# Rotation tables of a recurrence: built in one array from powers 1 to 64, the negative half copied backwards

## The chip, the cores and the metric

The kernel runs on one core of a Trainium2 chip. The metric is the device time in microseconds of one execution of the whole program; lower is better.

## The reference, cut to what matters

One layer of an encoder with 1024 prompt and 256 sample tokens, all in float32: a feed-forward half step, a mixing sublayer of two head groups, a second feed-forward half step. One head group is a diagonal complex recurrence (S5), forward and backward in time:

```python
ar = mag * jnp.cos(lam_im * step)
ai = mag * jnp.sin(lam_im * step)
...
_, _, hr, hi = lax.associative_scan(_complex_linear_combine, (a_r, a_i, bur, bui), reverse=reverse, axis=0)
return jnp.einsum('lgp,ghp->lgh', hr, c_re) - jnp.einsum('lgp,ghp->lgh', hi, c_im)
```

The kernel cuts the tokens into chunks of 8: 128 chunks for the prompt and 32 for the sample. It takes the rotation out of the state from chunk to chunk, so that what is scanned has a real decay. For that it needs a table of cosine and sine of (chunk number x angle) for each of the 32 groups and 2 directions.

## The kernel before, in words

The program is one stream of work whose stages overlap. The first feed-forward half is done in two parts: four token tiles first (function `ffn`), then the six remaining prompt tiles (`ffn1_halves`, which calls `gated` and `Down.run`). `gated` goes over 22 slices of the hidden width. For each it makes seven block products (`p1` to `p7`) of twelve TensorE matmuls of 384 columns each (line 1435), into two sets of three PSUM banks in turn. Around the matmuls VectorE adds results out of PSUM (line 1456), ScalarE copies and applies the activation (1468, 1474, 1504), VectorE multiplies (1497, 1505). The weights of the next slices are split into a high and a low part by ScalarE (line 200) and VectorE (line 201), and GpSimd forms sums of weight blocks ahead of that (line 1403).

The preparation of the recurrence, `s5_mats`, is a generator that is run in turns with that part: `weave((fb, 33), (s5_mats(...), 102))` advances whichever of the two has the smaller share of its units behind it (33 and 102 units). Its first part makes the tables, in four passes of eight group pairs. A pass doubles the table seven times: `cmul` (lines 453 to 458, six VectorE operations) turns entries 0 to n-1 into entries n to 2n-1, for n = 1, 2, ..., 64, with cosine in one array and sine in another. Then ScalarE copies the first 32 entries behind the 128 (line 595), VectorE clears eight entries (596), ScalarE makes the negated sine (598), and ScalarE's queue issues eight stores of the finished arrays to DRAM (601). There is one buffer each for cosine, sine and negated sine, so the next pass writes them when the stores have landed. After each doubling and each pass stands a `yield 2`, so the tables take 64 of the 102 units. The second part makes the matrices of the recurrence (lines 605 to 676; VectorE operations on line 577, TensorE on 627, 649, 661 and 666). It first takes buffers that the tables have given back.

The order within each engine's queue is fixed when the program is built: each queue runs its instructions in that order, and an instruction that waits holds those behind it. Instructions of the tables may be placed ahead of their turn where their inputs are ready, and in the trace they are. `s5_prep`, which runs during the first part of the feed-forward half, makes the powers of two of the rotation by which the doublings multiply (lines 547 to 567).

Of the kernel before, what the change touches and what calls it, by code (L numbers as in the profile page):

```python
# [12 lines left out]
AF = mybir.ActivationFunctionType  # L13
ALU = mybir.AluOpType

D = 1024
DFF = 2816
NFT = DFF // 128
# [29 lines left out]
def bc(ap, axis, n):  # L48

    v = ap.unsqueeze(axis)  # L50
    shape = list(v.shape)
    shape[axis] = n
    return v.to_broadcast(shape)
# [396 lines left out]
def cmul(K, outr, outi, ar, ai, br, bi, t):  # L450

    V = K.nc.vector
    V.tensor_tensor(out=outr, in0=ar, in1=br, op=ALU.mult)
    V.tensor_tensor(out=t, in0=ai, in1=bi, op=ALU.mult)
    V.tensor_tensor(out=outr, in0=outr, in1=t, op=ALU.subtract)
    V.tensor_tensor(out=outi, in0=ar, in1=bi, op=ALU.mult)
    V.tensor_tensor(out=t, in0=ai, in1=br, op=ALU.mult)
    V.tensor_tensor(out=outi, in0=outi, in1=t, op=ALU.add)


def s5_prep(K, A, keep, banks):

    nc = K.nc
    V = nc.vector
    TT = lambda o, a, b, op: V.tensor_tensor(out=o, in0=a, in1=b, op=op)
# [67 lines left out]
    b01, b23, t = K.new(2, 64, 16), K.new(2, 64, 16), K.new(64, 16)  # L533
# [13 lines left out]

    yield 4

    tn = K.new(7, 2, 32)  # L550
    er, ei = tn.v[:, :, 0], tn.v[:, :, 1]
    for src, dst in ((e8r, er[:, 0]), (e8i, ei[:, 0])):
        ps = banks.get(32)
# [2 lines left out]
        nc.scalar.copy(out=dst, in_=ps)  # L556
    V.tensor_scalar(out=ei[:, 0, 16:32], in0=ei[:, 0, 16:32], scalar1=-1.0, scalar2=None, op0=ALU.mult)
    u = tq.v[:, 0, 0:32]
    for j in range(6):
        TT(er[:, j + 1], er[:, j], er[:, j], ALU.mult)  # L560
        TT(u, ei[:, j], ei[:, j], ALU.mult)
        TT(er[:, j + 1], er[:, j + 1], u, ALU.subtract)
        V.scalar_tensor_tensor(out=ei[:, j + 1], in0=er[:, j], scalar=2.0, in1=ei[:, j], op0=ALU.mult, op1=ALU.mult)
# [8 lines left out]
def s5_mats(K, A, keep, scr, cfg):  # L572


    nc = K.nc
    V = nc.vector
    TT = lambda o, a, b, op: V.tensor_tensor(out=o, in0=a, in1=b, op=op)
    g = lambda k: A[k][0]
    turn = K.new(7, 2, 32)
    nc.sync.dma_start(out=turn.v, in_=keep["turn"])  # L580
    er, ei = turn.v[:, :, 0], turn.v[:, :, 1]
    c_, s_, n_, tm = (K.ring(1, 8, n) for n in (160, 160, 160, 64))
    for j in range(0, 32, 8):
        d, q = divmod(j, 16)
        c, s, t = c_.get(), s_.get(), tm.get()
        V.memset(c[:, :, 0:1], 1.0)
        V.memset(s[:, :, 0:1], 0.0)
        for lev in range(7):
            n = 1 << lev
            cmul(K, c[:, :, n:2 * n], s[:, :, n:2 * n], c[:, :, 0:n], s[:, :, 0:n],  # L590
                 bc(er[:, lev, j:j + 8], 2, n), bc(ei[:, lev, j:j + 8], 2, n), t[:, :, 0:n])
            yield 2

        for v in (c, s):
            nc.scalar.copy(out=v[:, :, 128:160], in_=v[:, :, 0:32])
            V.memset(v[:, :, 127 + d:128 + d], 0.0)
        n = n_.get()
        nc.scalar.activation(out=n, in_=s, func=AF.Copy, scale=-1.0)
        for half, v, src in ((0, 0, c), (1, 0, c), (0, 1, n), (1, 1, s)):
            for gg in range(2):  # L600
                nc.scalar.dma_start(out=scr["tab"][half * 64:half * 64 + 64, q:q + 8, v, gg, d], in_=src[gg * 64:gg * 64 + 64])
        yield 2
    for r in (c_, s_, n_, tm, turn):
        r.free()

    banks, bank1 = Banks(K, cfg["prep"][:-1]), Banks(K, cfg["prep"][-1:])
    bs = K.new(2, 64, 16)
# [6 lines left out]
    for b in range(4):  # L614
        gv = gw.get()
        for d in (1, 0):
# [14 lines left out]
            for q in range(0, 8, 4):  # L631
                dg, gg = d * 32 + b * 8 + q, b * 8 + q

                def powers(lo, hi, rev):
                    r, i = (p[:, lo:hi, dg:dg + 4] for p in (pwr, pwi))
                    if rev:
                        r, i = r[:, ::-1], i[:, ::-1]
                    return tuple(bc(v.rearrange("p k g -> p g k"), 3, 16) for v in (r, i))

                iv, tv = inj.get(), tmp.get()[:, :, 0:8]  # L640
                r, i = powers(0, 8, d == 0)
# [12 lines left out]
                r, i = powers(0, 9, d == 1)  # L654
# [19 lines left out]
        for s in range(8):  # L674
            nc.sync.dma_start(out=scr["mat"][s * 16:s * 16 + 16, b * 8:b * 8 + 8, 4].rearrange("h g x -> g h x"),
                              in_=gv[:, 7 - s:15 - s].rearrange("p t h -> p (t h)"))
# [950 lines left out]
def weave(*gens):  # L1627

    live = [[0.0, n, g] for g, n in gens]
    while live:  # L1630
        w = min(live, key=lambda w: w[0] / w[1])
        try:
            w[0] += next(w[2]) or 1
        except StopIteration:
            live.remove(w)
# [7 lines left out]
def emit(ctx, tc, nc, A, dbg=None):  # L1643
    K = Ctx(ctx, tc, nc)
    V = nc.vector
    g = lambda k: A[k][0]
    dp = ctx.enter_context(tc.tile_pool(name="dr", bufs=1, space=bass.MemoryType.DRAM))
    shapes = {"mat": (128, 32, 5, 128), "tab": (128, 16, 2, 2, 2, 160), "u": (512, 8, 160), "g": (512, 8, 160),
              "rate": (2048,), "b": (128, 2, 64, 16), "turn": (128, 7, 2, 32), "h": (NFT, 128, 1024), "h1": (NFT, 128, 768), "x2": (128, 8, D)}
    for nm in NAMES:  # L1650
        L, NT, R = PARTS[nm]
        shapes.update({"spec_" + nm: (2, 2, L // R // 128, 128, 2, R, 256), "x1_" + nm: (128, NT, D), 
# [1 line left out]
    scr = {k: dp.tile(list(s), F32, name="scr_" + k) for k, s in shapes.items()}  # L1654
# [46 lines left out]
    def filter_spectra(ids):  # L1701

        FC = filt_consts(K, A)
        yield from filters(K, A, "sample", FC, scr, ids, {})
        yield from s5_prep(K, A, scr, Banks(K, ids[-2:]))
        yield from filters(K, A, "prompt", FC, scr, ids, {})

    out, x1T = {}, {}
# [16 lines left out]
    def ffn1_halves(N, first, tail, turn):  # L1725

        tb, src = Banks(K, (4, 5, 6, 7)), tokens(A["x_prompt"][0], "prompt")
        X = Blocks(K, N // 2, False)
        X.make(X.NAMES[0:2])
        xs = [K.new(2, D) for _ in range(N // 2)]  # L1730
        for j, x in enumerate(xs):
            for i in range(2):
                nc.sync.dma_start(out=x.v[:, i], in_=src[:, first + 2 * j + i])
            X.even(x.v, j, tb)
        G = GateUp(K, g("ffn1_w_gate"), g("ffn1_w_up"), True)
        G.load()
        yield 0.01
        G.early(0)
        G.parts(0)
        X.make(X.NAMES[2:])  # L1740

        def begin():
            G.sums(0, 0)
            G.sums(0, 1)
            G.load()
            G.load()
            for j, x in enumerate(xs):
                X.odd(x.v, j, tb)
                x.free()
            G.early(1)  # L1750

        dn = Down(K, g("ffn1_w_down"), scr["h1"], N)
        xr = []

        def spare(n):

            X.free(GateUp.OPS[n][1])
            if n in (1, 2):
                dn.load()
            elif n == 6:  # L1760
                xr.append(Parts(K, N, D))
                for s in range(N):
                    nc.sync.dma_start(out=xr[0].at(s), in_=src[:, first + s])

        yield from gated(K, X, G, scr["h1"], ((0, 1, 2), (3, 4, 5)), begin, spare, True)

        def done(s):
            nc.sync.dma_start(out=scr["x1_prompt"][:, first + s], in_=xr[0].at(s))
            turn(xr[0], s)

        yield from dn.run(xr[0], g("ln1_g"), g("ln1_b"), range(6), done, tail=tail)
        xr[0].free()

    fb = ffn1_halves(6, 2, to_mix, turn1)
# [7 lines left out]
    nc.sync.dma_start(out=gains[:, 0:4], in_=g("ssm_norm_g").rearrange("(k p) -> p k", p=128))  # L1782
    nc.sync.dma_start(out=gains[:, 4:8], in_=g("hy_norm_g").rearrange("(k p) -> p k", p=128))
    weave((fa, 33), (filter_spectra((4, 5, 6, 7)), 183))
    weave((fb, 33), (s5_mats(K, A, scr, scr, dict(prep=(6, 7))), 102))


    xs = load_x([(scr["x1_sample"], s) for s in range(2)])
# [8 lines left out]
    x2, x2T, yT = {}, {}, {nm: [] for nm in NAMES}  # L1797
# [231 lines left out]
```

## Time and profile before

| | us |
|---|---|
| median of 3 runs (lowest, highest) | 2573.36 (2571.69, 2576.63) |
| the profiled execution's own time | 2577.11 |
| its span, first to last instruction | 2575.3 |

The profile is of one execution. TensorE is PE (weight loads are PEld), VectorE is DVE, ScalarE is ACT, GpSimd is POOL. Starts are microseconds from the span's start. A line number is that of the kernel; a helper's line stands for all who call it. "idle before" is time in which the engine had nothing running just before the instruction, and what ended it stands behind it. PEclk is the clock that was granted to TensorE, as a share of the full 2.4 GHz.

### The profile page before, as it was taken

The page shows a single profiled execution, that of the slowest core. Times are in us where ns is not written, and L with a number is a line of the kernel's source. Part 1 is how long each engine was busy: PE and PEld are TensorE (multiplying, and loading weights), DVE is VectorE, ACT ScalarE, POOL GpSimd, SP SyncE. Part 2 cuts the span into 40 slices and gives each one's busy share as a digit, 9 for nine tenths or more (in the row PEclk, how much of TensorE's full clock was granted, in tenths as well). Part 3 has the DMA queues.
Part 4 walks back from the last instruction along what each step waited for, and adds up shares of the span by engine and source line. Part 5 has one row for each costly group of instructions (what it writes and reads, how often), then busy time and mean ns, then how long its engine had stood idle before and what let it go on. Part 6 is the DMA issues. An engine that isn't in the chain of part 4 may idle for free.

```text
span 2575.3 us, 32433 instructions
## 1 busy us (share of the span) xinstructions
PE 2485.9 (97%) x12605; PEld 2119.3 (82%) x12605; DVE 1897.0 (74%) x2873; ACT 867.3 (34%) x1291; POOL 221.4 (9%) x158
## 2 busy tenths in 40 slices
PE   8999999889999999999999999999989999999998
PEld 6777777779999988788888878899768888888887
DVE  6887777689886697657896788788986566556437
ACT  5434443323333332123444313333332222223200
POOL 0000000244343100000000000000230000000001
PEclk9999999999999999999999999999999999999999
DMA  7333232444563464445556654565433223244301
GB/s 206 114 117 94 94 93 84 155 118 131 152 168 97 166 208 144 147 135 156 172 173 189 223 196 140 168 189 160 140 112 95 77 78 95 74 149 186 130 35 66
DMA packets 358705, 349.43 MB, mean 136 GB/s; under 512 B 41260, under 2 KB 308421, under 8 KB 357526
## 3 DMA queue, kind: packets, MB, share of 16 engines
q1 hardware_dynamic: 323510, 328.99, 40.8%
q10 hardware_dynamic: 35040, 18.35, 2.8%
q8 instruction: 99, 1.62, 0.3%
q14 instruction: 56, 0.46, 0.1%
HBM read 262.64 MB, written 84.39 MB: 135 GB/s over the span
## 4 chain that ended last, share of the span: by engine, by line
PE 69%; DVE 18%; DMA 5%; issue 3%; ACT 2%; POOL 2%; SPq 0%; ACTq 0%; DVEq 0%; POOLq 0%
PE banks L1435 22%; PE banks L1601 14%; PE banks L327 10%; PE banks L360 6%; DVE s L201 4%; DVE s L965 3%; PE banks L895 3%; PE banks L1277 3%; PE banks L812 3%; PE banks L1099 2%; ACT s L200 1%; DVE s L780 1%; PE banks L1152 1%; DVE s L1013 1%; DMA s<-in_ffn_w_gate_dram 1%
## 5 line engine op out<-in xcount | busy, mean ns | idle before, releaser
L1435 PE MATMUL banks<-s,s 128*128 128x512 f32 (+1 forms) x3544 | 751.5, 367 | 12.3 <-DVE s L1456 8.2
L200 ACT ACTIVATE s<-s 128x1024 fp32r<-128x1024 f32 (+4 forms) x533 | 481.1, 915 | 827.5 <-PE banks L1435 207.2
L1435 PEld LDWEIGHTS banks<-s,s 128*128 128x128 f32 x3544 | 650.1, 190 | 88.8 <-DVE s L1456 10.7
L201 DVE TENSOR_TENSOR s<-s,s 128x1024 fp32r<-128x1024 f32 (+4 forms) x533 | 570.8, 1081 | 194.7 <-ACT s L200 192.5
L327 PE MATMUL banks<-s,s 128*128 128x512 f32 (+1 forms) x2112 | 398.3, 341 | 2.5 <-ACT s L200 2.0
L1601 PE MATMUL banks<-s,s 128*128 128x512 f32 x1232 | 389.7, 395 | 0.6 <-DVE s L201 0.6
L327 PEld LDWEIGHTS banks<-s,s 128*128 128x128 f32 x2112 | 323.2, 190 | 52.6 <-issue 8.9
L1601 PEld LDWEIGHTS banks<-s,s 128*128 128x128 f32 x1232 | 231.7, 189 | 48.1 <-DVE s L201 1.4
L1601 PE MATMUL banks<-s 128*128 128x512 f32 x616 | 243.1, 396 | 0.0
L895 PE MATMUL banks<-s,s 128*128 128x512 f32 (+1 forms) x1152 | 237.8, 361 | 0.6 <-DVE s L201 0.6
L1456 DVE TENSOR_TENSOR s<-banks,s 128x384 f32<-128x384 f32 (+1 forms) x220 | 135.5, 619 | 129.0 <-PE banks L1435 125.6
L895 PEld LDWEIGHTS banks<-s,s 128*128 128x128 f32 x1152 | 188.4, 190 | 28.8 <-DVE s L201 1.1
L360 PE MATMUL banks<-s,s 128*128 128x512 f32 x792 | 198.3, 396 | 2.1 <-DVE s L201 1.2
L259 POOL TENSOR_TENSOR cst<-cst 128x1 f32<-128x1 f32 (+2 forms) x38 | 48.7, 1283 | 1655.4 <-DVE cst L258 1655.4
L1607 DVE TENSOR_TENSOR s<-banks,s 128x512 f32<-128x512 f32 x140 | 95.8, 687 | 121.3 <-PE banks L1601 121.2
L360 PEld LDWEIGHTS banks<-s,s 128*128 128x128 f32 x792 | 146.4, 190 | 34.3 <-issue 1.9
L1601 PEld LDWEIGHTS banks<-s 128*128 128x128 f32 x616 | 116.2, 189 | 23.2
L1277 PE MATMUL banks<-s,s 128*128 128x512 f32 x480 | 122.8, 405 | 4.0 <-DVE s L1199 1.6
L1403 POOL TENSOR_TENSOR s<-s 128x512 f32<-128x512 f32 x44 | 68.4, 1559 | 673.8 <-DMA s<-in_ffn_w_up_dram 500.2
L1277 PEld LDWEIGHTS banks<-s,s 128*128 128x128 f32 x480 | 89.8, 190 | 23.6 <-DVE s L1199 2.1
L714 DVE TENSOR_TENSOR s<-banks,s 128x512 f32<-128x512 f32 (+2 forms) x112 | 58.8, 550 | 39.8 <-ACT s L831 20.7
L812 PEld LDWEIGHTS banks<-s,s 128*128 128x128 f32 x624 | 81.0, 190 | 7.1 <-ACT s L200 2.5
(218 smaller groups left out, 2536.8 us busy)
## 6 DMA issues: line engine op xcount, KB each, us to landing
s<-in_ffn_w_gate_dram SPq DMA_DIRECT2D x88, 512.0 KB
s<-in_ffn_w_up_dram SPq DMA_DIRECT2D x88, 512.0 KB
s<-in_ffn_w_down_dram SPq DMA_DIRECT2D x88, 512.0 KB
scr_h<-s SPq DMA_DIRECT2D x22, 512.0 KB
s<-scr_h SPq DMA_DIRECT2D x22, 512.0 KB
scr_tab<-s ACTq DMA_DIRECT2D x32, 320.0 KB
s<-scr_mat SPq DMA_DIRECT2D x16, 640.0 KB
s<-scr_tab SPq DMA_DIRECT2D x16, 640.0 KB
```

The lines of the kernel that those rows point to most:

```text
L200: K.nc.scalar.activation(out=hi, in_=src, func=AF.Copy)
L201: K.nc.vector.tensor_tensor(out=lo, in0=src, in1=hi.bitcast(F32), op=ALU.subtract)
L327: nc.tensor.matmul(pss[-1][c], lhsT=w[:, wv, d], rhs=xT.parts[k][c].at(d), start=(d == 0 and wv == 0 and k == 0), stop=(d == 7 and wv == 1))
L360: nc.tensor.matmul(ps, lhsT=h[s // 4][:, a, s % 4 * 128:(s % 4 + 1) * 128], rhs=w[:, b, dh * 512:(dh + 1) * 512], start=(n == 0), stop=(n ...
L812: nc.tensor.matmul(ps, lhsT=F[kt][a].v[:, s, i], rhs=b.v[:, s], start=(n == 0), stop=(n == 3 * NT // R - 1))
L895: nc.tensor.matmul(p, lhsT=w[:, wv, d], rhs=xT[nm].parts[k][c].at(d), start=(d == 0 and wv == 0 and k == 0), stop=(d == 7 and wv == 1))
L965: TT = lambda o, a, b, op: V.tensor_tensor(out=o, in0=a, in1=b, op=op)
L1277: nc.tensor.matmul(ps, lhsT=y[s // per][a].v[:, k, ts], rhs=W[k].v[:, b, dh * 512:dh * 512 + 512], start=(k == 0 and a == 0 and b == 0), s ...
L1435: self.K.nc.tensor.matmul(ps, lhsT=w[i][:, d], rhs=x[k][:, d], start=first and m == 0, stop=m == len(todo) - 1, skip_group_check=True)
L1456: TT = lambda o, a, b: V.tensor_tensor(out=o, in0=a, in1=b, op=ALU.add)
L1601: nc.tensor.matmul(ps, lhsT=p[a].v[:, o:o + 128], rhs=p[b].v[:, dh * 512:dh * 512 + 512], start=m == 0, stop=m == len(todo) - 1)
L1607: nc.vector.tensor_tensor(out=xv, in0=ps, in1=xv, op=ALU.add)
```

## The change

The tables run from chunk -64 to 63, where they ran from 0 to 127. One array holds cosine and sine of entries 0 to 64. Six doublings, of three operations each over both halves of the array, make entries 2 to 64 from entry 1, which is a copy of the angle's own cosine and sine. Entries 64 to 127 of the finished table are a copy of entries 0 to 63 by ScalarE, entries 0 to 63 are a copy of entries 64 to 1 read backwards, with the sign of the sine turned. This is done for three finished arrays (cosine, negated sine, sine) in two buffers that take turns; eight stores per pass remain. The angle powers are six where they were seven, and a copy of their sines with both signs is made by ScalarE. Yields per pass are seven where they were eight, and the weight of `s5_mats` in the weave is 95 where it was 102.

```diff
-    tn = K.new(7, 2, 32)
+    tn = K.new(6, 2, 32)
...
-    for j in range(6):
+    for j in range(5):
         TT(er[:, j + 1], er[:, j], er[:, j], ALU.mult)
...
-    turn = K.new(7, 2, 32)
+    turn = K.new(6, 2, 32)
     nc.sync.dma_start(out=turn.v, in_=keep["turn"])
-    er, ei = turn.v[:, :, 0], turn.v[:, :, 1]
-    c_, s_, n_, tm = (K.ring(1, 8, n) for n in (160, 160, 160, 64))
+    er, es = turn.v[:, :, 0], K.new(6, 2, 32)
+    for i, sign in ((0, -1.0), (1, 1.0)):
+        nc.scalar.activation(out=es.v[:, :, i], in_=turn.v[:, :, 1], func=AF.Copy, scale=sign)
+    pos, out, tm = K.new(2, 8, 65), K.ring(2, 8, 160), K.new(2, 8, 32)
+    p = pos.v
+    V.memset(p[:, 0, :, 0:1], 1.0)
+    V.memset(p[:, 1, :, 0:1], 0.0)
     for j in range(0, 32, 8):
         d, q = divmod(j, 16)
-        c, s, t = c_.get(), s_.get(), tm.get()
-        V.memset(c[:, :, 0:1], 1.0)
-        V.memset(s[:, :, 0:1], 0.0)
-        for lev in range(7):
+        V.tensor_copy(out=p[:, :, :, 1], in_=turn.v[:, 0, :, j:j + 8])
+        for lev in range(6):
             n = 1 << lev
-            cmul(K, c[:, :, n:2 * n], s[:, :, n:2 * n], c[:, :, 0:n], s[:, :, 0:n],
-                 bc(er[:, lev, j:j + 8], 2, n), bc(ei[:, lev, j:j + 8], 2, n), t[:, :, 0:n])
+            t, o, i = tm.v[:, :, :, 0:n], p[:, :, :, n + 1:2 * n + 1], p[:, :, :, 1:n + 1]
+            TT(t, i[:, ::-1], bc(es.v[:, lev, :, j:j + 8], 3, n), ALU.mult)
+            TT(o, i, bc(bc(er[:, lev, j:j + 8], 1, 2), 3, n), ALU.mult)
+            TT(o, o, t, ALU.add)
             yield 2
 
-        for v in (c, s):
-            nc.scalar.copy(out=v[:, :, 128:160], in_=v[:, :, 0:32])
-            V.memset(v[:, :, 127 + d:128 + d], 0.0)
-        n = n_.get()
-        nc.scalar.activation(out=n, in_=s, func=AF.Copy, scale=-1.0)
-        for half, v, src in ((0, 0, c), (1, 0, c), (0, 1, n), (1, 1, s)):
-            for gg in range(2):
-                nc.scalar.dma_start(out=scr["tab"][half * 64:half * 64 + 64, q:q + 8, v, gg, d], in_=src[gg * 64:gg * 64 + 64])
+
+        for i, sign, halves, v in ((0, 1.0, (0, 1), 0), (1, -1.0, (0,), 1), (1, 1.0, (1,), 1)):
+            o = out.get()
+            nc.scalar.activation(out=o[:, :, 64:128], in_=p[:, i, :, 0:64], func=AF.Copy, scale=sign)
+            rev = p[:, i, :, 1:65][:, :, ::-1]
+            nc.scalar.activation(out=o[:, :, 0:64], in_=rev, func=AF.Copy, scale=-sign if i else sign)
+            nc.scalar.copy(out=o[:, :, 128:160], in_=o[:, :, 0:32])
+            V.memset(o[:, :, 127 + d:128 + d], 0.0)
+            for half in halves:
+                for gg in range(2):
+                    nc.scalar.dma_start(out=scr["tab"][half * 64:half * 64 + 64, q:q + 8, v, gg, d], in_=o[gg * 64:gg * 64 + 64])
         yield 2
...
-    weave((fb, 33), (s5_mats(K, A, scr, scr, dict(prep=(6, 7))), 102))
+    weave((fb, 33), (s5_mats(K, A, scr, scr, dict(prep=(6, 7))), 95))
```

The scratch tensor `turn` in DRAM shrinks from seven to six entries along with it.

## Rows read from the trace of the kernel before

**Rows 1.** The page: busy time, share of the span and instructions of each engine.

```profile
PE 2485.9 (97%) x12605; PEld 2119.3 (82%) x12605; DVE 1897.0 (74%) x2873; ACT 867.3 (34%) x1291; POOL 221.4 (9%) x158
```

**Rows 2.** Busy time by stretch: stretch, its length, engines in turn, PEclk, DMA share, GB/s.

```profile
550.00:750.00 200.00, 186.18 (x1022) 183.13 (x1023) 172.22 (x358) 74.91 (x137) 77.45 (x51) 0.96 0.48 128
750.00:850.00 100.00, 98.87 (x569) 98.23 (x568) 67.48 (x101) 38.04 (x69) 41.56 (x29) 1.00 0.39 120
...
900.00:950.00 50.00, 49.59 (x246) 40.80 (x245) 46.48 (x60) 16.82 (x27) 0.00 (x0) 1.00 0.60 201
```

**Rows 3.** Busy time by stretch of line 1435 alone (PE, PEld, PEclk, DMA).

```profile
555.47:607.00 51.53, 48.70 (x267) 47.93 (x267) 0.95 0.43 112
607.00:655.00 48.00, 43.69 (x241) 42.98 (x240) 0.96 0.50 137
655.00:704.00 49.00, 44.98 (x244) 44.14 (x243) 0.93 0.51 135
704.00:752.00 48.00, 46.94 (x269) 46.13 (x268) 1.00 0.55 147
752.00:800.00 48.00, 48.00 (x279) 48.00 (x278) 1.00 0.54 164
```

**Rows 4.** Waits of PE, 500 to 1110: total us, times, longest us.

```profile
PE banks L1435 <- DVE s L1456: 13.1, 7, 4.0
```

**Rows 5.** Timeline of DVE at the end of the third pass: start, us, instruction.

```profile
688.19 1.78 DVE L453 TENSOR_TENSOR s<-s,s 128x512 f32<-128x512 f32 x1
...
694.48 0.54 DVE L1456 TENSOR_TENSOR s<-banks,s 128x384 f32<-128x384 f32 x1
```

**Rows 6.** Timeline of ACT there.

```profile
693.65 1.15 ACT L200 ACTIVATE s<-s 128x512 fp32r<-128x512 f32 x2 [8.03 <-DVE s L455]
```

**Rows 7.** Timeline of PE, 545 to 760, instructions that waited.

```profile
645.07 0.45 PE L1435 MATMUL banks<-s 128*128 128x384 f32 x1 [4.02 <-DVE s L1456]
695.07 15.12 PE L1435 MATMUL banks<-s,s 128*128 128x384 f32 x72 [3.99 <-DVE s L1456]
```

**Rows 8.** DVE by line, 555 to 760: busy us, mean ns, idle before.

```profile
L458 DVE TENSOR_TENSOR s<-s,s 128x8 f32<-128x8 f32 (+6 forms) x28 | 16.1, 575 | 0.0
...
L456 DVE TENSOR_TENSOR s<-s,s 128x8 f32<-128x8 f32 (+6 forms) x28 | 9.5, 339 | 1.3 <-DMA scr_tab<-s 1.3
```

**Rows 9.** DVE by line and shape, 555 to 760, same columns.

```profile
L456 DVE TENSOR_TENSOR s<-s,s 128x256 f32<-128x256 f32 x4 | 1.7, 414 | 0.0
...
L456 DVE TENSOR_TENSOR s<-s,s 128x16 f32<-128x16 f32 x4 | 0.7, 167 | 0.0
L456 DVE TENSOR_TENSOR s<-s,s 128x8 f32<-128x8 f32 x4 | 0.7, 164 | 1.3 <-DMA scr_tab<-s 1.3
```

**Rows 10.** Timeline of DVE in the first pass, its last doubling.

```profile
585.66 0.68 DVE L453 TENSOR_TENSOR s<-s,s 128x512 f32<-128x512 f32 x1
```

**Rows 11.** Line 1403, 550 to 860: duration ns min/median/max, first and last start.

```profile
L1403 POOL TENSOR_TENSOR s<-s x40: 1283/1295/5017, 557.2 to 853.8; 128x512 f32<-128x512 f32 x40
```

**Rows 12.** ACT by line and shape, 555 to 760, columns as in rows 8.

```profile
L200 ACT ACTIVATE s<-s 128x512 fp32r<-128x512 f32 x90 | 54.5, 627 | 80.2 <-PE banks L1435 49.1 <-POOL s L1403 22.5 <-DVE s L455 8.0
...
L598 ACT ACTIVATE s<-s 128x1280 f32<-128x1280 f32 x4 | 5.1, 1265 | 2.0 <-issue 2.0
L595 ACT COPY s<-s 128x256 f32<-128x256 f32 x8 | 3.3, 407 | 9.8 <-DVE s L455 5.2 <-DVE s L458 4.6
```

**Rows 13.** Timeline of ACT's queue: the first store of the first pass.

```profile
593.26 0.67 ACTq L601 DMA_DIRECT2D scr_tab<-s  x1
```

**Rows 14.** Chain that ended last, in order of time: its step through a store.

```profile
598.93 7.52 DMA scr_tab<-s
```

**Rows 15.** Waits of DVE, 500 to 1110, columns as in rows 4.

```profile
DVE s L586 <- DMA scr_tab<-s: 1.8, 1, 1.8
```

**Rows 16.** Waits of ACT, 500 to 1110.

```profile
ACT s L1504 <- DMA scr_tab<-s: 2.6, 1, 2.6
```

**Rows 17.** Line 577, the matrices of the recurrence, columns as in rows 11.

```profile
L577 DVE TENSOR_TENSOR s<-s,cst x64: 678/718/759, 864.5 to 1048.2; 128x512 f32<-128x512 f32 x32, 128x576 f32<-128x576 f32 x32
```

More of the change, by code (lines that the diff above doesn't have):

```diff
@@ L602, in s5_mats @@
         yield 2
-    for r in (c_, s_, n_, tm, turn):
-        r.free()
+    for b in (pos, out, tm, es, turn):
+        b.free()
     banks, bank1 = Banks(K, cfg["prep"][:-1]), Banks(K, cfg["prep"][-1:])
@@ L1648, in emit @@
     shapes = {"mat": (128, 32, 5, 128), "tab": (128, 16, 2, 2, 2, 160), "u": (512, 8, 160), "g": (512, 8, 160),
-              "rate": (2048,), "b": (128, 2, 64, 16), "turn": (128, 7, 2, 32), "h": (NFT, 128, 1024), "h1": (NFT, 128, 768), "x2": (128, 8, D)}
+              "rate": (2048,), "b": (128, 2, 64, 16), "turn": (128, 6, 2, 32), "h": (NFT, 128, 1024), "h1": (NFT, 128, 768), "x2": (128, 8, D)}
     for nm in NAMES:
```

## The prediction, made before the change was run

> **What bounds the kernel now.** I read the page first: TensorE is busy for 97% of the span [rows 1], so time can be won only where TensorE stands still or runs at less than its rate. Then the busy time by stretch. While the tables are made (550 to 750) VectorE is busy for 172.2 of 200 us and TensorE's granted clock is 0.96 on average (between its levels of 2.4 and 1.2 GHz); in the next 100 us, the same feed-forward code without table work, VectorE is busy for 67.5 of 100, TensorE for 98.9, at 1.00, which is 2.4 GHz [rows 2]. So the tables stand in the one stretch of this stage where TensorE loses time.
>
> How much it loses I take from counts of line 1435's matmuls, because a slow matmul also counts as busy. In 752 to 800 there are 279 in 48.00 us, 0.172 us each. At that rate the four stretches in front of it, one per table pass, would have held 299.5, 279, 284.9 and 279; they hold 267, 241, 244 and 269 [rows 3]. The missing 32.5, 38, 40.9 and 10 matmuls are 5.6 + 6.5 + 7.0 + 1.7 = 20.9 us. That is the pot. Of it, waits that the trace names, PE on VectorE's line 1456 (emptying a PSUM bank), are 13.1 us in seven [rows 4]; the rest is mostly the lower clock behind them.
>
> The reader can see one such loss being made. At 688 VectorE runs the last doubling of the third pass; its 512-element product takes 1.78 us, and the emptying of the bank starts only at 694.48 [rows 5]. ScalarE meanwhile stood for 8.03 us behind the table's stores, which wait for VectorE [rows 6]. PE resumes at 695.07 after 3.99 us; the second pass cost it 4.02 at 645 [rows 7].
>
> **Why a table operation is dear here.** The same 512-element product took 0.68 us in the first pass [rows 10] against 1.78 in the third [rows 5]. The difference is GpSimd's subtraction of line 1403, running beside it; those take 1.295 us at the median and up to 5.017 [rows 11], so each holds up the other. The Trainium skill (SBUF — State Buffer, section Who interferes with whom) says that a VectorE operation with two SBUF inputs contends with a GpSimd operation that reads SBUF, and the one that comes second waits for the other's whole length. The trace agrees, with 0.68 against 1.78 us.
>
> **The change, part by part.**
>
> Removed and added on VectorE. The six table lines, 28 operations each, are busy for 16.1 us (first line) down to 9.5 (last), 77.7 us over all six [rows 8]. Without collisions the six sizes from 8 to 256 elements take 0.164, 0.167, 0.182, 0.216, 0.281 and 0.414 us (the first, the second and the last of them in [rows 9]), and 512 takes 0.68 [rows 10]: 2.10 us per line and pass, times 6 lines and 4 passes, 50.5 us. The other 27.2 us are collisions. The new pass has three operations for each size from 16 to 512: 1.94 us x 3 x 4 = 23.3 us. Strides and broadcasts are as now; the swap of the two halves moves whole rows, so I cost it at nothing. Collisions shrink between the count (72 of 168, to 11.7) and not at all (27.2); I take the clean time's share, 12, since an operation meets GpSimd's in proportion to the time it runs. So VectorE has 35 us of table work instead of 77.7, 42 less (bounds 27 to 43). In 550 to 750 it would then be busy for about 130 of 200 us, 65%, the density of the stretch behind it in which PE loses about 1% [rows 2]. Memsets and the four small copies are hidden in VectorE's new idle time; without that cover they would cost under 1 us.
>
> What of the pot comes back. If the loss goes with the table's VectorE time, 54% of 20.9, 11.4 us. If it goes with a threshold (at 65% PE loses about what it loses in 750 to 850, 1.1 us in 100), 20.9 less 2.2, 18.7. None, if the loss follows single collisions that still fall as badly, 0. Rows 7 are losses at the end of a pass, when the six widest operations stand one behind the other, and those are halved in number and not gone; I stay nearer to proportion: **-13 us**.
>
> ScalarE. Now per pass two copies of 256 elements at 0.407 us and one of 1280 at 1.265 [rows 12]: 8.3 us in four passes. New are three times two of 512 (the split's form, 0.627) and one of 256: 5.0 us per pass, 20 us in all; a backwards read I price like the forward one (no row reads backwards on ScalarE; twice that for the reversed third would add 7.5 us, spread likewise). ScalarE goes from 74.9 to about 87 busy of 200 us [rows 2]: not a bound. But its copies stand in front of the bank copies and weight splits behind them, and each of the 12 arrays now makes a round (ScalarE copies, VectorE clears, ScalarE's queue issues) where there were two such rounds per pass. **+1 us**, bounds 0 and +8 (four passes, 2 us of wait each).
>
> Stores. Eight per pass as now, of the same size. What is late next: the third array of a pass reuses the buffer of the first, so a ScalarE copy, where now VectorE's next pass, waits for four stores to land. That is the slower rival below; in the sum, 0.
>
> The matrices move. The tables take 56 of 95 units where they took 64 of 102. In the weave's count that is 0.589 x 33 = 19.45 units of the feed-forward part, and 19.7 after its next yield, against 20.71 and, by its yield, 21.1. So the second part of `s5_mats` starts 1.4 units earlier, about 20 us at 84 x 0.172 = 14.5 us per unit. Its 0.7-us VectorE operations start at 864.5 now [rows 17], just behind GpSimd's last (853.8) [rows 11]; they would begin inside GpSimd's work. In 900 to 950 VectorE is at 46.5 of 50 and PE still at 49.6, with GpSimd idle [rows 2]: it is the collisions that cost. At the tables' rate, 20.9 us lost in 197, 20 us of overlap costs **+2 us** (0 to +5). Their end also comes about half a unit earlier, with the loads queued behind their last stores: 0, at best -4.
>
> The angle powers lose four operations of 32 elements, between 0.167 and 0.414 us each [rows 9], under a filter stage; the smaller `turn` transfer is one of each kind: 0, and under 1 us uncovered.
>
> **Sum:** -13 + 1 + 2 = -10 us. Against the profiled execution's own 2577.1 that is 2567.1; that one stood 3.8 above the median of the runs, so for the median 2573.4 - 10 = **2563 us**. What is won here passes through to the end, as the stages behind are PE's too [rows 1]. A measurement of this kernel tells about 0.2%, 5.1 us, from no change.
>
> **The rivals.**
>
> A. *The whole pot comes back.* For it: 65% is the density at which PE hardly loses. Against: rows 7 show losses made by a queue of a few wide operations, which no average forbids. Gain 17 to 22 us, 2552 to 2556. Chance 0.14.
>
> B. *Nothing to be measured.* TensorE is at 97%, and VectorE has idle time in the span as a whole; the gaps of 4 us come back where the matrices now meet GpSimd, or in the new rounds. Say 20 x 0.2 at the matrices, 8 at the rounds: -13 + 4 + 8 = -1, 2572 (within 5.1 us). Against: in this stage PE's gaps name VectorE [rows 4]. Chance 0.24. The Trainium skill (Perfetto Trace Analysis, Identifying the Most-Contended Engine) says to improve the engine of highest occupancy, by which a cut on VectorE would give 0 here, 2573; the same page allows regimes in which the engine changes, and rows 2 show one.
>
> C. *Slower: ScalarE held at the third array.* The first store of a pass is issued at 593.26 [rows 13]; the step of the chain that begins with the fourth, at 598.93, lasts 7.52 us [rows 14], so the four have landed 13.2 us after the first issue. Between them ScalarE's queue has the second array (1.7 us) and some stores (six at about 0.6): if the third array's copy comes next, ScalarE stands for about 8 us, four times. A stand of 8.03 [rows 6] went with a stretch that lost 7.0 us, so 4 x 7 = 28: -10 + 28 = +18, 2591. It decides from 2.5 us lost per pass. For it: the queue is in order. Against: now the same waits on these stores cost VectorE only 1.8 + 1.3 us [rows 9, 15] and ScalarE 2.6 [rows 16], since other work was placed in front. Chance 0.14, half of it below 2585.
>
> **How the numbers follow.** My forecast, a gain of 5.1 to 17, has 0.48. Faster by over 0.2%: 0.48 + 0.14 = 0.62; within 0.2%: 0.24; slower: 0.14. The range leaves out the best of A and most of C: 2553 to 2577, from the threshold's full gain with a little besides to a loss of 4 us. The forecast alone runs from 2556 to 2568.
>
> **What would show it.** Right: six table lines become three with 72 operations and 30 to 40 us busy; VectorE in the table stage at 60 to 70%; the wait of line 1435 on line 1456 falls from 13.1 to under 6 us; stretches like rows 3 hold over 270 matmuls. The first operation of the matrices' line starts 20 to 35 us earlier. Wrong by C: ScalarE shows waits on the table's stores of several us in each pass, and the gaps of PE follow them. Wrong by B: fewer VectorE us, yet the same missing matmuls, or as many missing around the matrices' start. Wrong at a size: collisions do not shrink with the operations, and three lines take 45 us or more.

## The result and the profile after

The changed kernel took 2562.0 us (median of 10 runs, 2555.0 to 2566.5) against 2572.6 (2569.5 to 2578.1) before it: a ratio of 0.995, with a 95% interval of 0.9938 to 0.9962. Timed again it was 2560.9 against 2575.9, 0.9945 (0.993 to 0.996). So it is faster by 10.6 us in the one comparison and 15 in the other.

The two profiles differ by more: the span fell from 2575.3 to 2553.2. The profiled execution after is the fastest of its ten runs, that of before one of the slower. So nothing below rests on the two spans; it rests on stretches, and on the second profile where it matters. The page of after, first part:

```profile
span 2553.2 us, 32335 instructions
PE 2475.8 (97%) x12605; PEld 2111.5 (83%) x12605; DVE 1874.3 (73%) x2775; ACT 878.4 (34%) x1317; POOL 216.3 (8%) x158
```

Over the whole program VectorE has 98 instructions fewer and is busy for 22.7 us less. The busy time by stretch, as in [rows 2]:

```profile
550.00:750.00 200.00, 195.07 (x1105) 193.69 (x1105) 158.06 (x276) 89.52 (x168) 78.62 (x55) 0.99 0.55 155
750.00:850.00 100.00, 98.75 (x571) 98.05 (x570) 68.23 (x102) 39.30 (x76) 36.89 (x26) 1.00 0.28 86
```

The matmuls of the feed-forward part (line 1443 after, 1435 before) by the stretches of [rows 3]:

```profile
555.47:607.00 51.53, 48.33 (x267) 47.27 (x265) 0.97 0.48 128
607.00:655.00 48.00, 46.73 (x269) 46.73 (x270) 1.00 0.54 152
655.00:704.00 49.00, 48.54 (x280) 48.23 (x280) 1.00 0.63 177
704.00:752.00 48.00, 48.00 (x279) 48.00 (x278) 1.00 0.52 154
752.00:800.00 48.00, 48.00 (x279) 48.00 (x278) 1.00 0.32 94
```

At 0.172 us each, 32.5, 10, 4.9 and 0 are missing, 8.1 us where before 20.9 were. The stretch of the first pass holds no more matmuls than before in this profile (267 in both; 275 in the second), the next two hold 28 and 36 more, and the granted clock of the second and third rose from 0.96 and 0.93 to 1.00. The wait of these matmuls on VectorE's emptying of the banks (line 1464 after, 1456 before), as in [rows 4], went from 13.1 us to 5.8, the longest from 4.0 to 2.1:

```profile
PE banks L1443 <- DVE s L1464: 5.8, 5, 2.1
```

The wait of 2.1 us that is left stands at the end of the first pass. On VectorE the emptying of the bank (L1464) comes behind the last five table operations of the pass, two of 256 and three of 512 elements (a row of several is named by its first):

```profile
568.80 3.54 DVE L577 TENSOR_TENSOR s<-s,s 128x256 f32<-128x256 f32 x3
572.27 0.68 DVE L201 TENSOR_TENSOR s<-s,s 128x512 fp32r<-128x512 f32 x1
572.87 2.35 DVE L577 TENSOR_TENSOR s<-s,s 128x512 f32<-128x512 f32 x2
575.15 0.54 DVE L1464 TENSOR_TENSOR s<-banks,s 128x384 f32<-128x384 f32 x1
```

```profile
575.75 0.50 PE L1443 MATMUL banks<-s 128*128 128x384 f32 x1 [2.06 <-DVE s L1464]
```

So the loss that [rows 7] show at the end of a pass is still there, at half its size.

The 72 table operations by size (VectorE by line and shape, 545 to 760):

```profile
L577 DVE TENSOR_TENSOR s<-s,s 128x512 f32<-128x512 f32 x12 | 12.1, 1007 | 0.2
L577 DVE TENSOR_TENSOR s<-s,s 128x256 f32<-128x256 f32 x12 | 10.0, 845 | 0.2
L577 DVE TENSOR_TENSOR s<-s,s 128x16 f32<-128x16 f32 x12 | 5.0, 449 | 0.3
L577 DVE TENSOR_TENSOR s<-s,s 128x64 f32<-128x64 f32 x12 | 3.5, 313 | 0.2
L577 DVE TENSOR_TENSOR s<-s,s 128x128 f32<-128x128 f32 x12 | 3.2, 290 | 0.3
L577 DVE TENSOR_TENSOR s<-s,s 128x32 f32<-128x32 f32 x12 | 3.1, 284 | 0.2
```

They sum to 36.9 us, of which 13.6 are over the 23.3 of the clean durations: collisions are still there, some 9 us on the two widest forms and 3 us on the narrowest (449 ns, where 167 are clean). ScalarE's new copies, and their waits (ACT by line, 555 to 760, columns as in [rows 12]):

```profile
L602 ACT ACTIVATE s<-s 128x512 f32<-128x512 f32 x12 | 7.5, 626 | 11.5 <-DVE s L577 7.4 <-issue 3.2 <-DMA scr_tab<-s 1.0
L604 ACT ACTIVATE s<-s 128x512 f32<-128x512 f32 x12 | 7.5, 625 | 0.0
...
L605 ACT COPY s<-s 128x256 f32<-128x256 f32 x12 | 4.7, 394 | 0.1
```

The copy that reads backwards (604) costs what the forward one does, 625 against 626 ns. ScalarE's wait on a store before a buffer is written again is 1.0 us in all.

**Where the time went, by stage.** The table below takes two lengths from each profile: from the first to the last matmul of lines 1435/1443 (the gated part, in which the tables are made), and from there to the last of 1601/1609 (the down part). For the two kernels these are the rows of those lines, first and last start at their end:

```profile
L1435 PE MATMUL banks<-s,s x1696: 332/334/687, 534.7 to 894.3; 128*128 128x384 f32 x189
L1435 PE MATMUL banks<-s x152: 333/334/522, 534.5 to 894.0; 128*128 128x384 f32 x152
...
L1601 PE MATMUL banks<-s,s x528: 387/389/776, 889.6 to 1109.3; 128*128 128x512 f32 x176
```

```profile
L1443 PE MATMUL banks<-s,s x1696: 331/334/525, 530.3 to 879.9; 128*128 128x384 f32 x189
L1443 PE MATMUL banks<-s x152: 333/334/525, 530.1 to 879.6; 128*128 128x384 f32 x152
...
L1609 PE MATMUL banks<-s,s x528: 387/389/482, 880.8 to 1088.5; 128*128 128x512 f32 x176
```

| kernel | gated part, us | down part, us | ratio to before (95%) |
|---|---|---|---|
| before | 359.8 | 215.0 | 1 |
| after; second profile | 349.8; 348.4 | 208.6; 210.5 | 0.995 (0.9938 to 0.9962); 0.9945 (0.993 to 0.996) |
| e1_pace | 361.8 | 210.9 | 0.9997 (0.9987 to 1.0007) |
| e2_oldpace | 345.8 | 215.1 | 0.9932 (0.9919 to 0.9945) |
| e3_nodoubling | 343.6 | 213.2 | 0.9918 (0.9904 to 0.9933) |
| e4_ring3 | 349.6 | 208.1 | 0.9933 (0.992 to 0.9946) |
| e5_twice | 362.2 | 210.3 | 0.9993 (0.9984 to 1.0002) |
| e6_before_nosum | 333.8 | 213.7 | 0.9881 (0.986 to 0.9901) |
| e7_after_nosum | 336.3 | 210.3 | 0.9877 (0.9859 to 0.9895) |
| e8_nocopies | 355.4 | 208.3 | 0.9973 (0.996 to 0.9986) |
| e9_psum | 346.5 | 213.6 | 0.9941 (0.9925 to 0.9957) |
| e10_ring3_oldpace | 344.4 | 213.9 | 0.9938 (0.9922 to 0.9955) |
| e11_vector_sums | 337.4 | 208.4 | 0.987 (0.9854 to 0.9887) |

Outside these two parts the profiles hardly differ: from the last matmul of the down part to the end, all fourteen profiles lie between 1462.9 and 1468.3 us. The start of the gated part wanders from 527.8 to 536.5, with no relation to the change.

### The profile page after: what moved, and what is told of

Read it like the earlier page. It is cut to its first block, busy times and chain, and to the rows that moved or that the text cites. A ratio compares the mean times of both kernels' runs of the same rounds, so it can differ in the third digit from the quotient of the medians.

```text
span 2553.2 us, 32335 instructions
## 1 busy us (share of the span) xinstructions
PE 2475.8 (97%) x12605; PEld 2111.5 (83%) x12605; DVE 1874.3 (73%) x2775; ACT 878.4 (34%) x1317; POOL 216.3 (8%) x158
## 4 chain that ended last, share of the span: by engine, by line
PE 74%; DVE 15%; DMA 4%; issue 3%; ACT 2%; POOL 1%; SPq 0%; DVEq 0%; ACTq 0%; POOLq 0%
PE banks L1443 25%; PE banks L1609 15%; PE banks L327 10%; PE banks L360 6%; PE banks L903 3%; PE banks L1285 3%; DVE s L973 3%; PE banks L820 3%; DVE s L201 3%; PE banks L1107 2%; DMA s<-in_ffn_w_gate_dram 1%; ACT s L200 1%; DVE s L788 1%; DVE s L577 1%; DVE s L1021 1%
## 5 line engine op out<-in xcount | busy, mean ns | idle before, releaser
L201 DVE TENSOR_TENSOR s<-s,s 128x1024 fp32r<-128x1024 f32 (+4 forms) x533 | 576.6, 1093 | 195.9 <-ACT s L200 193.2
L1464 DVE TENSOR_TENSOR s<-banks,s 128x384 f32<-128x384 f32 (+1 forms) x220 | 135.5, 620 | 135.3 <-PE banks L1443 133.6
L1411 POOL TENSOR_TENSOR s<-s 128x512 f32<-128x512 f32 x44 | 62.9, 1434 | 665.5 <-DMA s<-in_ffn_w_up_dram 495.6
```

The lines of the kernel that those rows point to most:

```text
L201: K.nc.vector.tensor_tensor(out=lo, in0=src, in1=hi.bitcast(F32), op=ALU.subtract)
L1464: TT = lambda o, a, b: V.tensor_tensor(out=o, in0=a, in1=b, op=ALU.add)
```

## The experiments

**The weave alone.** `e1_pace` is before with the last doubling's yield left out and the weight of 95.

```diff
-            yield 2
+            if lev < 6:
+                yield 2
...
-    weave((fb, 33), (s5_mats(K, A, scr, scr, dict(prep=(6, 7))), 102))
+    weave((fb, 33), (s5_mats(K, A, scr, scr, dict(prep=(6, 7))), 95))
```

> The tables of before, seven doublings and all, but with the weave of the change: seven yields per pass and a weight of 95, so that the matrices start as early as after the change. If the gain is VectorE's table work (my theory), nothing is won: 2570 to 2580 against 2573 before, the matrices starting some 20 us earlier and the missing matmuls of the table stage staying near 21 us. If the gain is the earlier start of the matrices, this run has it: 2562 to 2566.

It took 2574.7 against 2575.9: nothing is won. PE waits on VectorE's emptying of banks as before (13.3 us, the longest 4.0). The gated part is 2 us longer and the down part 4 us shorter: TensorE's own work for the matrices moves from the one into the other (its matmuls for them are busy for 2.9 us of the gated part before and for 6.7 in e1).

**The old weave under the new tables.** `e2_oldpace` is after with one more `yield 2` per pass and the weight of 102.

> The changed tables with the weave of before: eight yields per pass and a weight of 102. My theory: the table stage keeps its gain and the two us for the matrices among GpSimd's work come back, 2558 to 2564. If the gain is the earlier start of the matrices: 2570 to 2576, as before.

2558.1, ratio 0.9932: the gain needs nothing of the weave. The gated part shrinks from 359.8 to 345.8, 14.0 us; against after it is 3 us shorter there and 5 to 6 longer in the down part. In time, e2's interval overlaps that of after.

**How much the doublings cost in all.** `e3_nodoubling` leaves the doublings out of before; the tables are constants, and what else a pass does stays, but for its two clears on VectorE, which now cover whole arrays (1.1 us each).

```diff
-        V.memset(c[:, :, 0:1], 1.0)
-        V.memset(s[:, :, 0:1], 0.0)
+        V.memset(c, 1.0)
+        V.memset(s, 0.0)
...
-            cmul(K, c[:, :, n:2 * n], s[:, :, n:2 * n], c[:, :, 0:n], s[:, :, 0:n],
-                 bc(er[:, lev, j:j + 8], 2, n), bc(ei[:, lev, j:j + 8], 2, n), t[:, :, 0:n])
```

> Before with the doublings left out (the tables are constants; copies, stores, yields and weights stay). This measures the pot. My theory: the missing matmuls in 555 to 752 fall from 21 to 2 to 6 us and the time to 2553 to 2560. If the gaps of PE come from ScalarE's part or GpSimd's alone and not from VectorE's table work, the time stays at 2567 to 2576.

2553.1, ratio 0.9918, 21 us below before by the ratio (17 to 25 by its interval). The stretches of line 1433 (before's 1435) hold, as in [rows 3]:

```profile
555.47:607.00 51.53, 50.74 (x292) 50.26 (x291) 1.00 0.64 171
607.00:655.00 48.00, 48.00 (x278) 48.00 (x278) 1.00 0.83 228
655.00:704.00 49.00, 49.00 (x285) 49.00 (x284) 1.00 0.30 89
```

7.5 and 1 matmul are missing from the first two, 1.5 us: the pot of 20.9 us was the doublings' own, all but this.

**After, once more.**

> The changed kernel once more, for a second profile and its time on the chip of the three others. 2558 to 2566. The table stage should again lose 8 to 12 us of matmuls between 550 and 850, where before lost 25; what this profile and the first do not share (the start of the stage, the last weights' part) is taken as run to run.

Its gated part is 348.4 us long (349.8 in the first profile), its down part 210.5 (208.6). Between 550 and 850 it holds within six matmuls per 50 us of the first.

**A third buffer.** `e4_ring3` is after with `K.ring(3, 8, 160)` in place of `K.ring(2, 8, 160)`.

> The changed kernel with three buffers for the finished arrays in place of two, so that no array of a pass waits for the stores of an earlier one of the same pass. If the wait on the stores costs little, as the profile after says (1.0 us of ScalarE), 2559 to 2565, as after. If ScalarE is held there, 2552 to 2557.

2556.7, ratio 0.9933 (0.992 to 0.9946). The gated part is that of after, 349.6 us against 349.8 and 348.4: the stores do not hold ScalarE. The time itself fell into the range that was set for the other outcome; it lies 4 us below after_again's, and the intervals of the two overlap.

**VectorE's table work put back.** `e5_twice` does every table operation of after a second time, into a buffer that nobody reads.

```diff
+    dmy = K.new(2, 8, 32)
...
             TT(o, o, t, ALU.add)
+            x = dmy.v[:, :, :, 0:n]
+            TT(x, i[:, ::-1], bc(es.v[:, lev, :, j:j + 8], 3, n), ALU.mult)
+            TT(x, i, bc(bc(er[:, lev, j:j + 8], 1, 2), 3, n), ALU.mult)
+            TT(x, o, t, ALU.add)
```

> The changed kernel with every table operation of VectorE done a second time into a buffer that nobody reads, so that 144 operations run in place of 72: VectorE's table time goes back to 60 to 75 us, with all else of the change in place. If the loss goes with VectorE's table time: 2568 to 2574, most of the gain gone. If the gain comes from the buffers (no store to wait for before the next pass), the copies on ScalarE or the weave: 2560 to 2565.

2574.0, ratio 0.9993: the whole gain is gone, with the new buffers, copies, stores and weave in place. VectorE by line (555 to 760), and the waits of PE, as in [rows 4] (line 1448 is 1443 of after):

```profile
L577 DVE TENSOR_TENSOR s<-s,s 128x16 f32<-128x16 f32 (+5 forms) x144 | 65.2, 489 | 1.1
```

```profile
PE banks L1448 <- DVE s L1469: 13.4, 7, 4.1
```

65.2 us of table time bring back a wait of 13.4 us, where 77.7 had 13.1 and 36.9 have 5.8. The four stretches of [rows 3] hold 259, 256, 252 and 259 matmuls, so 20.0 us are missing.

**Without GpSimd's sums.** `e6_before_nosum` and `e7_after_nosum` are before and after without the subtractions and additions of line 1403 (1411 after); what waits for their results then waits for nothing.

> Before with GpSimd's sums of weight blocks left out (their buffers are zero). If a table operation is dear because it collides with GpSimd: the table lines take 50 to 54 us where they took 78, the missing matmuls of the table stage fall to under 6 us, and the time is 2545 to 2562. If VectorE's load alone is the cause, the stage still loses 15 us or more and the time is 2562 to 2572.

> The changed kernel with GpSimd's sums left out in the same way, to be read beside the one before. If collisions are what the change saves, the two differ by 0 to 4 us. If VectorE's load alone counts, they differ by 8 to 12 us as the full kernels do.

2543.1 (2 us below its range) and 2544.9: the change is worth nothing when GpSimd stands still. In e6 the table lines take 51 us, and the 512-element product of line 457 takes 684 ns (1192 before); the stretches, as in [rows 2]:

```profile
550.00:750.00 200.00, 200.00 (x1156) 199.90 (x1155) 149.91 (x368) 84.21 (x149) 0.00 (x0) 1.00 0.58 158
750.00:850.00 100.00, 100.00 (x579) 100.00 (x578) 56.01 (x95) 37.24 (x67) 0.00 (x0) 1.00 0.30 97
```

TensorE does not lose a matmul, with all 168 table operations of before in the stage. The sums are missing altogether here, and with them all waiting for their results; e11 below keeps the sums and loses nothing either.

**Without ScalarE's copies.** `e8_nocopies` cuts the three copies of an array down to one of 16 columns, and has GpSimd clear the two buffers first.

```diff
+    for b in out.bufs:
+        nc.gpsimd.memset(b.v, 0.0)
...
-            nc.scalar.activation(out=o[:, :, 64:128], in_=p[:, i, :, 0:64], func=AF.Copy, scale=sign)
-            rev = p[:, i, :, 1:65][:, :, ::-1]
-            nc.scalar.activation(out=o[:, :, 0:64], in_=rev, func=AF.Copy, scale=-sign if i else sign)
-            nc.scalar.copy(out=o[:, :, 128:160], in_=o[:, :, 0:32])
+            nc.scalar.activation(out=o[:, :, 64:80], in_=p[:, i, :, 0:16], func=AF.Copy, scale=sign)
```

> The changed kernel with ScalarE's copies of the tables reduced to one of 16 columns per group and array, so that the round of ScalarE, VectorE and store stays but 20 us of ScalarE's copying go (the arrays are otherwise zero). If the copies cost what I forecast, 1 us: 2558 to 2563, as after. If ScalarE's copies are what keeps the change from the whole pot: 2552 to 2557.

A miss: 2567.2, ratio 0.9973 (0.996 to 0.9986), some 5 us slower than after, whose intervals it just touches. The timeline of VectorE, of GpSimd and of PE in its first pass:

```profile
561.85 1.29 DVE L577 TENSOR_TENSOR s<-s,s 128x32 f32<-128x32 f32 x1
563.06 0.68 DVE L201 TENSOR_TENSOR s<-s,s 128x512 fp32r<-128x512 f32 x1
563.66 3.87 DVE L577 TENSOR_TENSOR s<-s,s 128x32 f32<-128x32 f32 x3
567.45 0.68 DVE L201 TENSOR_TENSOR s<-s,s 128x512 fp32r<-128x512 f32 x1
568.05 0.54 DVE L1463 TENSOR_TENSOR s<-banks,s 128x384 f32<-128x384 f32 x1
```

```profile
561.41 1.67 POOL L1410 TENSOR_TENSOR s<-s 128x512 f32<-128x512 f32 x1 [2.46 <-DVE s L201]
563.16 3.06 POOL L1410 TENSOR_TENSOR s<-s,s 128x512 f32<-128x512 f32 x2
566.18 1.26 POOL L1410 TENSOR_TENSOR s<-s 128x512 f32<-128x512 f32 x1
```

```profile
568.65 10.19 PE L1442 MATMUL banks<-s,s 128*128 128x384 f32 x48 [4.12 <-DVE s L1463]
```

Four small table operations (a row of several is named by its first; here 32 to 64 elements) take 5.2 us beside four sums, and the bank waits behind them. It shows how much the order of a queue can cost, some 4 us at one place. The run is not after with less work alone, though. GpSimd's clears run at 540 and 549 us, 1.2 us each, among its sums; and VectorE's clear (line 605), whose column the one copy no longer writes, waits for the stores in VectorE's queue. VectorE's emptyings and table operations have 6.0 us of such waits in front of them, where after has none, the longest here:

```profile
656.09 0.56 DVE L1463 TENSOR_TENSOR s<-banks,s 128x384 f32<-128x384 f32 x1 [4.27 <-DMA scr_tab<-s]
656.10 0.07 DVE L605 MEMSET s<- 128x8 f32 x1
```

PE has no gap at that place, so what made the kernel slower as a whole is not shown.

**Table work that cannot collide.** `e9_psum` is e2 with the array of powers in two PSUM banks unused in this stage, so that each table operation has one input in SBUF and one in PSUM. Entry 0 is no longer in the array, so VectorE writes it into each finished array (line 600).

```diff
-    pos, out, tm = K.new(2, 8, 65), K.ring(2, 8, 160), K.new(2, 8, 32)
-    p = pos.v
...
+    out, tm = K.ring(2, 8, 160), K.new(2, 8, 32)
+    p = shaped(K.ps[:, 6 * 512:8 * 512], (2, 8, 64))
...
+            V.memset(o[:, :, 64:65], 0.0 if i else 1.0)
```

> The changed tables with the weave of before, and the array of powers in PSUM (two banks that stand unused in this stage) in place of SBUF, so that each product and sum on VectorE has only one input in SBUF. If the cost of a table operation is a collision of two-SBUF-input operations with GpSimd's sums, none of the 72 takes over 1 us, the table line takes 23 to 27 us, and the time is 2551 to 2557, at or below the same kernel with SBUF (2558). If PSUM operands collide as well, or the loss is VectorE's load, 2557 to 2562.

2560.5, ratio 0.9941. Half a hit. No table operation takes over 0.70 us and they sum to 24.1 us, as expected; but the gated part (346.5) is no shorter than with SBUF (345.8), and the time is no lower. Its table line and its splits (line 201), the first as duration ns min/median/max, the second by line in 555 to 760:

```profile
L577 DVE TENSOR_TENSOR banks<-banks,s x48: 172/258/699, 555.1 to 686.9; 128x16 f32<-128x16 f32 x8, 128x32 f32<-128x32 f32 x8, 128x64 f32<-128x64 f32 x8, 128x128 f32<-128x128 f32 x8
```

```profile
L201 DVE TENSOR_TENSOR s<-s,s 128x512 fp32r<-128x512 f32 x99 | 83.7, 857 | 31.6 <-ACT s L200 31.1
```

The splits take 857 ns each here, 837 in e2, 843 after, 844 without any doublings, 768 before, and 686 without GpSimd's sums. Where tables leave GpSimd's way, the splits meet it more. But from e2 to e9 that is 20 ns on 99 splits, 2 us, where the tables lost some 13 us of collisions: it is not the whole reason why the stage got no shorter. PE still waits for 6.4 us, in eight places (6.6 in six in e2). The trace shows a part of what remains. The written entry 0 waits for the stores in VectorE's queue:

```profile
DVE s L600 <- DMA scr_tab<-s: 7.7, 3, 3.9
```

and one wait of PE, 1.1 us at 695, follows such a stand. Three more, of 0.84 us each, at 740, 770 and 801, lie behind the last table operation (686.9): two sums of GpSimd take 3.4 us beside a split of 1.59, ScalarE waits 3.8 us for GpSimd, VectorE 3.2 us for ScalarE, and then a split of 1.22 us beside the next sum stands in front of the emptying. The split and PE's wait at 770:

```profile
768.60 1.22 DVE L201 TENSOR_TENSOR s<-s,s 128x512 fp32r<-128x512 f32 x1 [3.21 <-ACT s L200]
770.34 12.75 PE L1443 MATMUL banks<-s,s 128*128 128x384 f32 x72 [0.84 <-DVE s L1464]
```

So e9 shows that a table operation with one input in PSUM does not slow beside the sums; it does not price the collisions.

**The two edits together.** `e10_ring3_oldpace` is e2 with three buffers.

> The changed tables with three buffers for the finished arrays and the weave of before, the two single edits that came out 4 us below the changed kernel each. If they add up: 2551 to 2555. If both are the same 4 us, or run to run: 2555 to 2561.

2558.9, ratio 0.9938: they do not add up; the small differences among after, e2, e4 and e10 are not told apart by these runs.

**GpSimd's sums on VectorE.** `e11_vector_sums` is after with one word changed.

```diff
-            self.K.nc.gpsimd.tensor_tensor(out=o, in0=a, in1=b, op=op)
+            self.K.nc.vector.tensor_tensor(out=o, in0=a, in1=b, op=op)
```

> The changed kernel with the 88 sums of weight blocks moved from GpSimd to VectorE, nothing left out. They add 88 x 0.68 = 60 us to VectorE in a stage of 350 us, where it is busy for about 70%, and end every collision there; the splits of line 201 then take 0.60 us apart where they wait now. If the collisions are what costs, and not VectorE's load: 2545 to 2554, below the changed kernel. If VectorE's load counts in the same way (some 85% busy, as before the change): 2562 to 2575.

2542.6 against 2575.0, ratio 0.987 (0.9854 to 0.9887): below both kernels and 2 us below its range, and the lowest of all. The stretches, as in [rows 2]:

```profile
550.00:750.00 200.00, 200.00 (x1155) 199.90 (x1155) 169.86 (x345) 93.17 (x175) 0.00 (x0) 1.00 0.57 156
750.00:850.00 100.00, 100.00 (x584) 99.62 (x583) 76.87 (x129) 38.63 (x74) 0.00 (x0) 1.00 0.31 97
```

VectorE is busy for 169.9 of 200 us, nearly the 172.2 of before [rows 2], and PE loses nothing where it lost 14 us. The splits take 686 ns.

## Why the prediction was right, point by point

**The pot.** 20.9 us of missing matmuls, laid to the tables. Right: without the doublings 1.5 are missing, and the time falls by 21 us.

**VectorE's table time.** 35 us were forecast, bounds 35 to 51; 36.9 were measured, so the collisions did shrink with the time (13.6 left of 27.2, forecast 12).

**What comes back, -13 us.** The missing matmuls of the four stretches fell from 20.9 to 8.1 us, by 12.8; with the weave unchanged the gated part fell by 14.0. That VectorE's table time is the cause is shown by e5, where doubling the new work alone takes the whole gain back, and by e1, where the weave alone gives none. That it takes GpSimd's sums, and that VectorE's load alone costs nothing, is shown by e6, e7 and e11. Load is not out of it where the sums run: of the 28 us that e5 adds to the table lines 23.3 are the clean durations of its operations, and what VectorE's tables and splits take over their clean durations did not grow (some 29 us after, 28 in e5), yet the loss came back. It goes roughly with the table's VectorE time beside the sums: 36.9 us went with 8.1 missing, 65.2 with 20.0 and 77.7 with 20.9. Proportion was the bound of 11.4 that I stayed near. The step from there to -13 was a judgement between two bounds that no row decided, so that it met 12.8 is in part luck.

**The density of 65%.** This step was wrong, though the sum did not hang on it: VectorE is busy for 158 of 200 us, 79%. Two things took much of the freed time: more of the feed-forward part fits into the stretch (70 emptyings of a bank in 555 to 760, where 64 were), and the splits are slower, 843 ns against 768, since they now meet the sums that the tables met. A third is in the counting: operations that follow one another overlap in the trace by some 0.08 us (561.85 + 1.29 against 563.06, shown above at e8), so 77.7 us of table durations were less than that in busy time. So a threshold of load, one of my two bounds, was no sound way to size the gain. e11 runs at 85% and loses nothing.

**ScalarE, +1 us.** Not confirmed. The stores held it for 1.0 us; the run without the copies came out slower and changed more than the copies (e8). So the cost of the copies stays unmeasured. The backwards read is no dearer than the forward one.

**The matrices, +2 us.** Their first operation with a constant input, as in [rows 17]:

```profile
L577 DVE TENSOR_TENSOR s<-s,cst x64: 677/746/1778, 839.0 to 1021.2; 128x512 f32<-128x512 f32 x32, 128x576 f32<-128x576 f32 x32
```

It starts at 839.0, 25 us earlier (20 were forecast), the longest now takes 1.778 us, and the gated part is 3 us longer than with the old weave. But those 3 us are not collisions: behind 760 PE waits on VectorE's emptyings for 0.9 us in both kernels, and TensorE's own matmuls for the matrices are busy for 6.7 us of the gated part where they are for 3.0 in e2. The down part is 4 to 6 us shorter, for which I had allowed "at best -4" and summed 0. The two cancel within what can be timed: e2, with the old weave, is 3 us below after_again, and e1 is 1 us below before. So the term was given for a loss that the runs do not show.

**The rivals.** A, the whole pot: e3 is the pot, 0.9918, and after is at 0.995; it came near only in the gated part, where the change with the old weave won 14.0 of the 16.2 us that leaving the doublings out wins. B, nothing: refuted by the interval. I read [rows 2] there as a stretch in which the busiest engine changes; they do not show that, for TensorE is busy for 186.2 us and VectorE for 172.2. The gain came from waits of the busiest engine on one less busy. C, ScalarE held at the third array: refuted by the wait of 1.0 us and by e4, whose gated part is that of after.

**The sum.** -10 forecast, -10.6 measured in ten runs, and -14 to -15 in the later comparison; the terms of +1 and +2, which no run confirms, are within what the two comparisons leave open. Without them the sum would have been -13, which lies between the two, so the closeness of -10 to -10.6 says little for them.

**The signs.** Met: 72 operations in 36.9 us, the wait at 5.8 us (6.0 in the second profile), the start 25 us earlier. Not met: VectorE at 79% where 60 to 70 were given, and 267 and 269 matmuls in the first two stretches where over 270 were.

## What to carry to other kernels

Where TensorE waits on VectorE, look at what one operation takes beside GpSimd and alone before counting VectorE's busy time: here 170 busy us in 200 cost nothing without collisions, and 172 cost 14 us with them. Taking work out of one party to a collision moves part of the collision to the next (tables to splits); moving the other party's work onto VectorE, dearer as it looks by load, ended it and won some 19 us more (0.987 against 0.995). And a stage's pace in a weave moves work between neighbours; take the sum over both before you call it a cost.

## What the runs showed of the hardware that I had not expected

That VectorE and GpSimd take turns was in the trace; that other VectorE operations meet GpSimd more when one kind meets it less was not: without the doublings the mean of line 201 rose from 768 to 844 ns. With one of the table's operands in PSUM, 128x512 operations ran at 0.68 to 0.70 us beside GpSimd, uncollided, and the gated part did not get shorter, for reasons that are only in part shown. And GpSimd's 88 sums of 128x512, 1.29 to 1.32 us each at the median, cost the program as a whole some 17 us beside the new tables (2562.0 with them, 2544.9 without) and 32 us beside the old ones (2575.6 and 2543.1). They cost time with no table work beside them too: without the doublings, the gated part is still 10 us longer than with the doublings and without the sums (343.6 against 333.8).
